# A two-layer decoder trunk in split float32: the first block by all eight products, 384-column blocks first, squares on VectorE, low parts between a norm's steps, buffers that wait for their own bytes

## The chip, the cores and the metric

The kernel runs on one core of a Trainium2 chip. The metric is the device time of one execution in microseconds (us); less is better. A core has five engines that run side by side, each through its own instructions in order: TensorE (PE in the profile; PEld is its loading of the stationary operand), VectorE (DVE), ScalarE (ACT), GpSimd (POOL) and SyncE (SP, which here only issues DMAs). Matmuls accumulate into PSUM, which has eight banks of 128 x 512 float32.

## The reference

x has 512 tokens and 1024 channels, float32. Two layers, each:

```python
x = x + 0.5 * swiglu(rmsnorm(x, ln_ffn1[l]), w_ffn1_gu[l], w_ffn1_down[l])
h = rmsnorm(x, ln_mix[l]);  z = h @ w_in[l]
u_pool, q, k, v, gate_logits = split(z)
a = pool_mixer(u_pool, ...) @ w_pool_branch[l]
b = swa_sink_attention(q, k, v, sinks[l]) @ w_attn_branch[l]
g_pool, g_attn = split(sigmoid(gate_logits))
x = x + (g_pool * a + g_attn * b) @ w_out[l]
x = x + 0.5 * swiglu(rmsnorm(x, ln_ffn2[l]), w_ffn2_gu[l], w_ffn2_down[l])
# swiglu(h): g, u = split(h @ w_gu);  (silu(g) * u) @ w_down
# rmsnorm(x, g): x * rsqrt(mean(x*x) + 1e-6) * g
```

The inner width of a SwiGLU is 2816, so that w_gu has 5632 columns: 2816 for the gate, 2816 for the up part.

## The kernel before

**Split float32.** Every matrix operand is written as a high part (a copy rounded to the fast float32 format, made by ScalarE) and a low part (the difference, made by VectorE). One product of 128 x 128 by 128 x n is three matmuls: high by high, high by low, low by high. `term` (line 272) writes them for most stages; `split` (line 134) makes the parts of an activation: a copy on ScalarE, then a subtraction on VectorE that waits for it.

**Layout.** x lies transposed in SBUF as eight tiles of 128 channels by 512 tokens (k = 0 to 7, "k-tiles").

**SwiGLU** (`ffn`, line 396). The 2816 columns go in six blocks, two to a group, `GROUPS = ((512, 512), (512, 512), (384, 384))` (line 26). A block computes gate and up of its n columns. It takes channels in halves (k-tiles 0 to 3 and 4 to 7), tokens in halves of 256, and gate and up as halves of columns, and uses a Strassen form: seven products instead of eight, named a11, s2, s1, s3, a12, s4, a22 (line 27, `ORDER`; the first block of a SwiGLU goes by `FIRST`, with a12 second). A product is 24 matmuls of n columns: 2 weight chunks (c) x 2 token tiles (q) x 2 k-tiles x 3. They accumulate in three pairs of banks (pt[1], pt[2], pt[3]). Their activation operands, B11, T1, T2, T3, T4, B21 and B22, are halves of the scaled x and differences of them; `Norm.split(k)` (line 315) makes them: for k < 4 B11 and T1, for k >= 4 B21 with B22, T2 with T3, and T4. Behind the products stand small steps on VectorE and ScalarE (p1, p2, q6, q7, p3, a22, lines 443 to 477). p1, behind a11, copies pt[1] to r, and in the first block calls the norm's sums; a12 accumulates on pt[1], so it waits for these copies. q7, behind s3, computes v = P2 - r and then v = v - P3; s4 accumulates on P3, so it waits for that. `turned` (line 490) transposes a finished 128 x n product through the banks pt_tp and pt_pv into hh and hl (high and low part), which the down projection reads; half of the products wait in the list `turns` until `turn()`, behind the next block's a11 or early in `down`.

**down** (line 505): after each group, eight output tiles m, each over the group's 8 (or 6) k-tiles: 24 (or 18) matmuls; then `done` adds half of it to x. In the last group of a SwiGLU `done` also calls `nxt.split(m)` and `nxt.square(m)` for the next norm and then `W.prep()`. Before a norm of a SwiGLU the order of m is `HALVES` = 0, 4, 1, 5, 2, 6, 3, 7.

**The norm's scale.** `square` (line 353): ScalarE squares x, and the squares are added up into ssq, on GpSimd for the norms before a SwiGLU (`halves`), on VectorE for those before the mixer. `sums` (line 363): PE adds ssq over the partitions with eight small matmuls into pt_tp, VectorE makes rstd of it.

**Weights** (class `Weights`, line 146). A plan lists the chunks of 128 x 1024 (or 768) in the order of use. `prep` (line 253), after each used chunk, prepares on: low parts up to 3 chunks ahead (`LO`, three buffers wl), sums of chunks for s2 and s4 on VectorE (`add_up`, buffers sums), high parts up to 4 ahead on ScalarE (`HI`, buffers wh), then loads (six buffers raw). Plain loads go through SP's queue; for s1 and s3 a second load adds up in DMA through GpSimd's queue.

**The mixer** (`mix`, line 552) ends with eight tiles m in the order HALVES of x += y @ w_out, 24 matmuls each, with `nxt.split`, `nxt.square` and `prep` behind each.

**Order.** The class `InOrder` (line 82) keeps each engine's instructions in the order in which the program writes them; no scheduler moves them. All instructions carry line 90, its call, in the profile, so groups are told by their tiles. Pools of buffers (hp, ep, er, sums, the banks pf in `ffn`; mp, rp, ps, psc in `mix`) are opened and closed by each stage.

**The start** (from line 826 on): the loads of x and of the first chunks are written out by hand, then all eight `split` with the first chunks' high and low parts between, then eight `square`; then the first `ffn`.

Of the kernel before, what the change touches and what calls it, by code (L numbers as in the profile page):

```python
# [18 lines left out]
P = 128  # L19
# [6 lines left out]
GROUPS = ((512, 512), (512, 512), (384, 384))  # L26
# [75 lines left out]
def trunk(ctx, tc, xT, consts, vecs, rows, w_g4, w_g3, w_d8, w_d6, w_qkv, w_u, w_pool, w_gate, w_br, w_out, out):  # L102
# [43 lines left out]
    class Weights:  # L146
# [3 lines left out]
        def __init__(self):  # L150
# [3 lines left out]
            for l in range(L):  # L154
                for f in range(2):
# [8 lines left out]
                    for gi, group in enumerate(GROUPS):  # L164
                        for i, n in enumerate(group):
                            w = w_g4[l, f, b] if n == 512 else w_g3[l, f, b - 4]
                            self.block(w, 2 * n, FIRST if b == 0 else ORDER)
                            b += 1
                        last = gi + 1 == len(GROUPS)
                        for m in (HALVES if f == 1 and last else range(KT)):  # L170
                            w = w_d6[l, f, m] if last else w_d8[l, f, gi, m]
                            self.add("dn", 2 * sum(group) // 2, w)
# [136 lines left out]
    class Norm:  # L309
# [5 lines left out]
        def split(self, k):  # L315
# [9 lines left out]
            if not self.halves:  # L325
                split(self.h[:, k, :], self.l[:, k, :], x[:, k, :], scale=g)
                return
            j = k % 4
            of = lambda i, n=1: (t[:, i:i + n, j, :] for t in (self.h, self.l))
            two = lambda t: t.rearrange("p (i t) -> p i t", t=HT)  # L330
            if k < 4:
                split(*of(B11), two(x[:, k, :])[:, 0:1, :], scale=g)
                d = temp("d")[:, :HT]
                nc.vector.tensor_tensor(out=d, in0=x[:, k, :HT], in1=x[:, k, HT:], op=ALU.subtract)
                split(*of(T1), two(d), scale=g)
                return
            xg, t, u = temp("xg"), temp("t23"), temp("t4")[:, :HT]
            gj = self.gain[:, j:j + 1]
            nc.scalar.activation(out=xg, in_=x[:, k, :], func=AF.Copy, scale=g)
            bh, bl = of(B21, 2)  # L340
            nc.scalar.copy(out=bh, in_=two(xg))
# [7 lines left out]
            nc.vector.tensor_tensor(out=bl, in0=two(xg), in1=bh.bitcast(F32), op=ALU.subtract)  # L349
            split(*of(T2, 2), two(t))  # L350
            split(*of(T4), two(u))

        def square(self, k):
# [42 lines left out]
    def ffn(ctx, nm, nxt, last):  # L396
        hp = ctx.enter_context(tc.tile_pool(name="hp", bufs=1))
        ep = ctx.enter_context(tc.tile_pool(name="ep", bufs=1))
        er = ctx.enter_context(tc.tile_pool(name="er", bufs=2))
        W.sums = ctx.enter_context(tc.tile_pool(name="sums", bufs=2))  # L400
        bank["mm"] = ctx.enter_context(tc.tile_pool(name="pf", bufs=6, space=PSUM))
        W.low(W.used + LO)
        W.add_up(W.used + HI + 1)
        W.high(W.used + HI)
        W.low(W.used + LO)
        W.load()
        turns = []

        def block(n, base, hid, order):
# [39 lines left out]
            def p2():  # L449
                sa.update(enumerate(new("sa")))  # L450
                each(lambda q: nc.scalar.activation(out=sa[q], in_=pt[1][q], func=AF.Silu, scale=rs(q)))

            def q6():
                u2.update(enumerate(new("u")))
                each(lambda q: nc.vector.tensor_tensor(out=u2[q], in0=r1[q], in1=pt[2][q], op=ALU.subtract))

            def q7():
# [21 lines left out]
            steps = {"a11": (B11, 1, p1), "s2": (T2, 2, q6), "s1": (T1, 3, None), "s3": (T3, 2, q7),  # L479
                     "a12": (B21, 1, p2), "s4": (B22, 3, p3), "a22": (T4, 2, a22)}  # L480
# [19 lines left out]
        def turn():  # L500
            for t in turns:
                turned(*t)
            turns.clear()

        def down(hid, kts, final, ms):
# [7 lines left out]
            def done(m, pd):  # L513
# [3 lines left out]
                if final:  # L517
                    if nxt is not None:
                        nxt.split(m)
                        nxt.square(m)  # L520
                    if last:
                        nc.sync.dma_start(out=out[m * P:(m + 1) * P, :], in_=x[:, m, :])
# [16 lines left out]
        for gi, group in enumerate(GROUPS):  # L539
            hid = [hp.tile([P, 8, S], F32R, name=n) for n in ("hh", "hl")]  # L540
            base = 0
            for i, n in enumerate(group):
                block(n, base, hid, FIRST if gi == i == 0 else ORDER)
# [8 lines left out]
    def mix(ctx, l, nm, nxt):  # L552
        mp = ctx.enter_context(tc.tile_pool(name="mp", bufs=1))
        rp = ctx.enter_context(tc.tile_pool(name="rp", bufs=RING))
        bank["mm"] = ctx.enter_context(tc.tile_pool(name="ps", bufs=4, space=PSUM))
        psc = ctx.enter_context(tc.tile_pool(name="psc", bufs=1, space=PSUM))
# [261 lines left out]
        for m in HALVES:  # L818
# [3 lines left out]
            nxt.split(m)  # L822
            nxt.square(m)
            W.prep()

    gain = lambda l, i: vec[:, l, i * KT:(i + 1) * KT]
    nm = Norm(gain(0, 0), True)
# [108 lines left out]
```

## Time and profile before

| | |
|---|---|
| time, median of 3 runs | 1981.16 us (1981.11 to 1984.77) |
| profiled execution | 1982.2 us, of it span 1980.2 us |
| mean granted TensorE clock | 0.988 |
| ScalarE busy | 852.2 us (43%) |
| GpSimd busy | 132.9 us (7%) |
| read from HBM | 254.81 MB |

The span runs from the first to the last instruction. The profile lists busy time of each engine, groups of instructions (operation, output<-inputs by the program's names, shapes, count, busy time, mean duration), and for each instruction the idle time of its engine in front of it with the engine and tile that ended it (`[24.09 <-POOL ssq L90]`). "x24" in a line of the timeline or of the chain of waits is a number of instructions merged into it. A matmul's own duration is longer than the distance to the next one, since matmuls are pipelined; its price is the distance.

### The profile page before, as it was taken

How to read it: one execution, taken by the hardware profiler on the slowest of the kernel's cores; microseconds unless marked ns; L12 is line 12 of the kernel's file. 1: busy time of each engine (PE TensorE's matmuls, PEld its weight loads, DVE VectorE, ACT ScalarE, POOL GpSimd, SP SyncE). 2: the span in 40 equal slices, each digit the busy share in tenths (PEclk: the TensorE clock that was granted, in tenths of full speed). 3: DMA queues.
4: the chain of work that ended last, by engine and by line, in shares of the span. 5: the costliest groups of instructions: out<-in, count | busy, mean ns of one | idle time of the engine just before them, and what ended most of it. 6: DMA issues, size and time to landing. Idle time of an engine off the chain costs nothing.

```text
span 1980.2 us, 24215 instructions
## 1 busy us (share of the span) xinstructions
PE 1920.4 (97%) x9240; PEld 1611.0 (81%) x9240; DVE 1304.4 (66%) x1884; ACT 852.2 (43%) x1286; POOL 132.9 (7%) x134
## 2 busy tenths in 40 slices
PE   3999999999999999999989999999999999999999
PEld 2788889897778788889868888898977877888897
DVE  5765747667756774756787476576765677657474
ACT  5433525445534542433454244244454454335242
POOL 3000000000001100000020000000000021000000
PEclk6999999999999999999999999999999999999999
DMA  5655546422224554646546564553222237455452
GB/s 173 178 148 150 160 107 160 128 92 75 75 86 117 149 160 128 181 120 148 134 119 179 140 172 124 127 154 119 90 64 86 85 87 204 139 151 165 117 157 78
DMA packets 77348, 258.48 MB, mean 131 GB/s; under 512 B 8720, under 2 KB 8720, under 8 KB 77232
## 3 DMA queue, kind: packets, MB, share of 16 engines
q1 hardware_dynamic: 63072, 210.27, 32.6%
q0 software_dynamic: 13872, 46.28, 13.9%
q8 instruction: 72, 1.18, 0.3%
q14 instruction: 44, 0.36, 0.1%
q10 hardware_dynamic: 288, 0.39, 0.1%
HBM read 254.81 MB, written 2.10 MB: 130 GB/s over the span
## 4 chain that ended last, share of the span: by engine, by line
PE 92%; DVE 5%; ACT 2%; issue 0%; DMA 0%; POOL 0%; SPq 0%; ACTq 0%; POOLq 0%
PE mm L90 86%; PE sc L90 3%; PE pt_pv L90 2%; PE pt_tp L90 2%; DVE wl L90 2%; DVE xgl L90 1%; ACT xgh L90 1%; DVE x L90 1%; DVE t L90 1%; DMA raw<-in_w_g 0%; DVE ssq L90 0%; ACT wh L90 0%; POOL ssq L90 0%; DVE v L90 0%; ACT xg L90 0%
## 5 line engine op out<-in xcount | busy, mean ns | idle before, releaser
L90 ACT CAST wh<-raw 128x1024 fp32r<-128x1024 f32 (+1 forms) x420 | 417.9, 995 | 567.6 <-PE mm L90 536.3
L90 DVE TENSOR_TENSOR wl<-raw,wh 128x1024 fp32r<-128x1024 f32 (+1 forms) x420 | 495.2, 1179 | 158.7 <-PE mm L90 83.3
L90 PE MATMUL mm<-wh,xgh 128*128 128x512 f32 (+2 forms) x1440 | 532.4, 370 | 25.4 <-DVE x L90 9.0
L90 PE MATMUL mm<-wl,xgh 128*128 128x512 f32 (+2 forms) x1440 | 529.1, 367 | 1.2 <-DVE wl L90 1.2
L90 PE MATMUL mm<-wh,xgl 128*128 128x512 f32 (+2 forms) x1440 | 528.7, 367 | 0.0
L90 PEld LDWEIGHTS mm<-wh,xgh 128*128 128x128 f32 x1440 | 272.7, 189 | 64.4 <-ACT wh L90 21.7
L90 PEld LDWEIGHTS mm<-wl,xgh 128*128 128x128 f32 x1440 | 272.8, 189 | 37.3 <-DVE wl L90 2.0
L90 PEld LDWEIGHTS mm<-wh,xgl 128*128 128x128 f32 x1440 | 272.6, 189 | 35.8
L90 PE MATMUL mm<-hh,wl 128*128 128x512 f32 x704 | 279.9, 398 | 2.6 <-DVE wl L90 2.6
L90 PE MATMUL mm<-hh,wh 128*128 128x512 f32 x704 | 281.6, 400 | 0.0
L90 PE MATMUL mm<-hl,wh 128*128 128x512 f32 x704 | 279.5, 397 | 0.0
L90 DVE SCALAR_TENSOR_TENSOR x<-mm,x 128x512 f32<-128x512 f32 x96 | 66.3, 690 | 215.3 <-PE mm L90 215.3
L90 POOL DMA_DIRECT2D raw<-in_w_g x96 | 82.1, 858 | 1700.9 <-DMA raw<-in_w_g 757.2
L90 ACT CAST wh<-sums 128x1024 fp32r<-128x1024 f32 (+1 forms) x96 | 94.1, 980 | 197.6 <-PE mm L90 140.7
L90 PEld LDWEIGHTS mm<-hh,wl 128*128 128x128 f32 x704 | 133.0, 189 | 35.8 <-DVE wl L90 3.5
L90 PEld LDWEIGHTS mm<-hh,wh 128*128 128x128 f32 x704 | 133.0, 189 | 31.2
L90 PEld LDWEIGHTS mm<-hl,wh 128*128 128x128 f32 x704 | 132.9, 189 | 31.3
L90 PE MATMUL mm<-xgh,wh 128*128 128x512 f32 x384 | 154.8, 403 | 1.8 <-DVE x L90 1.8
L90 PE MATMUL mm<-xgh,wl 128*128 128x512 f32 x384 | 150.1, 391 | 0.0
L90 PE MATMUL mm<-xgl,wh 128*128 128x512 f32 x384 | 149.9, 390 | 0.0
L90 DVE TENSOR_TENSOR wl<-sums,wh 128x1024 fp32r<-128x1024 f32 (+1 forms) x96 | 106.7, 1131 | 12.8 <-PE mm L90 12.6
L90 PEld LDWEIGHTS mm<-xgh,wh 128*128 128x128 f32 x384 | 72.1, 188 | 22.5 <-issue 8.2
(174 smaller groups left out, 1979.6 us busy)
## 6 DMA issues: line engine op xcount, KB each, us to landing
raw<-in_w_g SPq DMA_DIRECT2D x160, 512.0 KB, 3.9
raw<-in_w_g POOLq DMA_DIRECT2D x64, 512.0 KB, 6.2
raw<-in_w_d SPq DMA_DIRECT2D x64, 512.0 KB, 3.4
raw<-in_w_g SPq DMA_DIRECT2D x80, 384.0 KB, 3.2
raw<-in_w_gate SPq DMA_DIRECT2D x32, 512.0 KB, 3.5
raw<-in_w_g POOLq DMA_DIRECT2D x32, 384.0 KB, 5.1
raw<-in_w_d SPq DMA_DIRECT2D x32, 384.0 KB, 3.1
raw<-in_w_br SPq DMA_DIRECT2D x16, 512.0 KB, 3.5
```

The source lines that it names most:

```text
L90: return lambda *args, **kw: self.tc.keep_in_program_order(call(*args, **kw))
```

## The change

- **First block plain.** In the first SwiGLU of layer 0 the first block is made by all eight products (`plain`), straight from the halves of x (`split_plain`), first all gate columns, then all up columns, with accumulators for four token tiles at once; pt_tp and pt_pv are two of them in the second half. The differences T1 to T4, which the later blocks need, are made behind the four chunks of the second half (`first`, `others`). The first chunk comes in two loads.
- **384-column blocks first.** `GROUPS` starts with (384, 384); the last group, behind which the next norm's operands are made, is (512, 512).
- **Squares on VectorE** before every norm.
- **Low parts between a norm's steps.** `split` gets a function `between`, called between the high part on ScalarE and the low part on VectorE; in `done` and at the end of the mixer it is `W.prep`.
- **v** takes P3 in a step p5 behind s1 (v = r + P3), and q7 becomes v = P2 - v. The norm's sums move from behind a11 to behind the first block's second kind with a step q6 (s2); two of `turns` are transposed behind each of the first two products.
- **Buffers that wait for their own bytes.** The pools of `ffn` and `mix` get `reuse_waits="tile"`; without it a pool that is opened on another's memory waits for the whole earlier pool.

```diff
-GROUPS = ((512, 512), (512, 512), (384, 384))
+GROUPS = ((384, 384), (512, 512), (512, 512))
...
-    def split(hi, lo, src, scale=None):
+    def split(hi, lo, src, scale=None, between=lambda: None):
         if scale is None:
             nc.scalar.copy(out=hi, in_=src)
+            between()
             nc.vector.tensor_tensor(out=lo, in0=src, in1=hi.bitcast(F32), op=ALU.subtract)
...
+                            plain = l == f == 0
+                            if plain and b == 0:
+                                for j in range(2):
+                                    for c in range(4):
+                                        self.add("plain", 2 * n, w[j, c])
+                            else:
+                                self.block(w, 2 * n, FIRST if b == int(plain) else ORDER)
...
+            else:
+                xg = self.scaled(k)
+                bh, bl = self.of(B21, k - 4, 2)
+                nc.scalar.copy(out=bh, in_=halves(xg))
+                between()
+                self.others(k - 4, xg, lambda: nc.vector.tensor_tensor(
+                    out=bl, in0=halves(xg), in1=bh.bitcast(F32), op=ALU.subtract
+                ))
...
+        def split_plain(self, k, b12):
...
+            if k < 4:
+                split(*self.of(B11, k), halves(x[:, k, :])[:, 0:1, :], scale=g)
+                split(*(t[:, k:k + 1, :] for t in b12), halves(x[:, k, :])[:, 1:2, :], scale=g)
+            else:
+                split(*self.of(B21, k - 4, 2), halves(x[:, k, :]), scale=g)
...
-                e = nc.gpsimd if self.halves else nc.vector
-                e.tensor_tensor(out=self.acc, in0=self.acc, in1=sq, op=ALU.add)
+                nc.vector.tensor_tensor(out=self.acc, in0=self.acc, in1=sq, op=ALU.add)
...
-        hp = ctx.enter_context(tc.tile_pool(name="hp", bufs=1))
+        hp = ctx.enter_context(tc.tile_pool(name="hp", bufs=1, reuse_waits="tile"))
...
             def p1():
                 r1.update(enumerate(new("r", er)))
                 each(lambda q: nc.scalar.copy(out=r1[q], in_=pt[1][q]))
-                if nm.rstd is None:
-                    nm.sums()
...
             def q6():
                 u2.update(enumerate(new("u")))
                 each(lambda q: nc.vector.tensor_tensor(out=u2[q], in0=r1[q], in1=pt[2][q], op=ALU.subtract))
+                if nm.rstd is None:
+                    nm.sums()
+                    gate()
+
+            def p5():
+                v.update(enumerate(new("v")))
+                each(lambda q: nc.vector.tensor_tensor(out=v[q], in0=r1[q], in1=pt[3][q], op=ALU.add))

             def q7():
-                v.update(enumerate(new("v")))
-                each(lambda q: nc.vector.tensor_tensor(out=v[q], in0=pt[2][q], in1=r1[q], op=ALU.subtract))
-                each(lambda q: nc.vector.tensor_tensor(out=v[q], in0=v[q], in1=pt[3][q], op=ALU.subtract))
+                each(lambda q: nc.vector.tensor_tensor(out=v[q], in0=pt[2][q], in1=v[q], op=ALU.subtract))
...
-                if kind == "a11":
+                if kind in order[:2]:
                     turn()
...
+        def plain(n, base, hid):
+            b12 = [sums.tile([P, 4 * HT], F32R, name="sums").rearrange("p (k t) -> p k t", k=4) for _ in range(2)]
+            pts = [mm()[:, :n] for _ in range(6)]
+            for k in range(KT):
+                nm.split_plain(k, b12)
+                if k % 2 == 0:
+                    W.high(k // 2 + 1)
+                    W.low(k // 2 + 1)
+            for k in range(KT):
+                nm.square(k)
+            act = []
+            for j in range(2):
+                if j:
+                    pts = pts[4:] + [pa.tile([P, S], F32, name=name)[:, :n] for name in ("pt_tp", "pt_pv")]
+                for c in range(4):
+                    wh, wl = (t[:, :2 * n].rearrange("p (k f) -> p k f", k=2) for t in W.take("plain"))
...
+                            term(pts[b], kt, KT, ah, al, wh[:, k, :], wl[:, k, :])
+                    if j == 0 and c == 3:
+                        nm.sums()
...
+                    W.prep()
+                    if j:
+                        nm.first(c)
+                        nm.others(c, nm.scaled(c + 4))
+            for b in range(NB):
+                u = (er if b < 2 else ep).tile([P, 512], F32, name=("r0", "r1", "v0", "v1")[b])[:, :n]
+                nc.vector.scalar_tensor_tensor(
+                    out=u, in0=pts[b], scalar=nm.rstd[:, b:b + 1], in1=act[b], op0=ALU.mult, op1=ALU.mult
+                )
+                turns.append((u, b, base, n, hid, b % 2))
...
-                if final:
-                    if nxt is not None:
-                        nxt.split(m)
-                        nxt.square(m)
+                if final and nxt is not None:
+                    nxt.split(m, W.prep)
+                    nxt.square(m)
+                    return
...
-    loads = iter(W.loads[2:RAW])
+    loads = iter(W.loads[1:RAW])
     for k in range(KT):
         nc.sync.dma_start(out=x[:, k, :], in_=xT[k * P:(k + 1) * P, :])
-        if k in (1, 3, 5):
+        if k < 2:
+            c = W.loads[0]
+            cols = slice(k * c["n"] // 2, (k + 1) * c["n"] // 2)
+            nc.sync.dma_start(out=c["raw"][:, cols], in_=c["src"][:, cols])
+        elif k % 2 == 0:
             W.issue(next(loads))
...
```

More of the change, by code (lines that the diff above doesn't have):

```diff
@@ L313, in __init__, with split @@
             self.h = self.rstd = None
-        def split(self, k):
+        def split(self, k, between=lambda: None):
             g = self.gain[:, k:k + 1]
@@ L325, in split, with of, scaled, first @@
             if not self.halves:
[L326 to L337, printed above, removed]
+                split(self.h[:, k, :], self.l[:, k, :], x[:, k, :], scale=g, between=between)
+            elif k < 4:
+                split(*self.of(B11, k), halves(x[:, k, :])[:, 0:1, :], scale=g, between=between)
+                self.first(k)
+            else:
+                xg = self.scaled(k)
+                bh, bl = self.of(B21, k - 4, 2)
+                nc.scalar.copy(out=bh, in_=halves(xg))
+                between()
+                self.others(k - 4, xg, lambda: nc.vector.tensor_tensor(
+                    out=bl, in0=halves(xg), in1=bh.bitcast(F32), op=ALU.subtract
+                ))
+        def of(self, i, j, n=1):
+            return [t[:, i:i + n, j, :] for t in (self.h, self.l)]
+        def scaled(self, k):
+            xg = temp("xg")
+            nc.scalar.activation(out=xg, in_=x[:, k, :], func=AF.Copy, scale=self.gain[:, k:k + 1])
+            return xg
+        def first(self, j):
+            d = temp("d")[:, :HT]
+            nc.vector.tensor_tensor(out=d, in0=x[:, j, :HT], in1=x[:, j, HT:], op=ALU.subtract)
+            split(*self.of(T1, j), halves(d), scale=self.gain[:, j:j + 1])
+        def others(self, j, xg, between=lambda: None):
+            t, u = temp("t23"), temp("t4")[:, :HT]
             gj = self.gain[:, j:j + 1]
-            nc.scalar.activation(out=xg, in_=x[:, k, :], func=AF.Copy, scale=g)
-            bh, bl = of(B21, 2)
-            nc.scalar.copy(out=bh, in_=two(xg))
             nc.vector.scalar_tensor_tensor(
@@ L348, in split @@
             nc.vector.tensor_tensor(out=u, in0=xg[:, :HT], in1=t[:, :HT], op=ALU.subtract)
-            nc.vector.tensor_tensor(out=bl, in0=two(xg), in1=bh.bitcast(F32), op=ALU.subtract)
-            split(*of(T2, 2), two(t))
-            split(*of(T4), two(u))
+            between()
+            split(*self.of(T2, j, 2), halves(t))
+            split(*self.of(T4, j), halves(u))
+        def split_plain(self, k, b12):
+            g = self.gain[:, k:k + 1]
+            if self.h is None:
+                self.h, self.l = (
+                    xp.tile([P, 7 * 4 * HT], F32R, name=n).rearrange("p (i k t) -> p i k t", i=7, k=4)
+                    for n in ("xgh", "xgl")
+                )
[4 more added lines that the diff above has]
+                split(*self.of(B21, k - 4, 2), halves(x[:, k, :]), scale=g)
         def square(self, k):
@@ L445, in p1, with gate @@
                 each(lambda q: nc.scalar.copy(out=r1[q], in_=pt[1][q]))
-                if nm.rstd is None:
-                    nm.sums()
             def p2():
+                if nm.rstd is not None:
+                    gate()
+            def gate():
                 sa.update(enumerate(new("sa")))
@@ L477, in a22 @@
                 ))
-            steps = {"a11": (B11, 1, p1), "s2": (T2, 2, q6), "s1": (T1, 3, None), "s3": (T3, 2, q7),
+            steps = {"a11": (B11, 1, p1), "s2": (T2, 2, q6), "s1": (T1, 3, p5), "s3": (T3, 2, q7),
                      "a12": (B21, 1, p2), "s4": (B22, 3, p3), "a22": (T4, 2, a22)}
@@ L542, in ffn @@
             for i, n in enumerate(group):
-                block(n, base, hid, FIRST if gi == i == 0 else ORDER)
+                if nm is first and gi == i == 0:
+                    plain(n, base, hid)
+                else:
+                    fresh = W.sums is None
+                    if fresh:
+                        open_sums()
+                    block(n, base, hid, FIRST if fresh else ORDER)
                 base += n // P
```

88 lines of the change are left out of this document (45 added, 43 removed).

## The prediction

> **What bounds the kernel now.** I read the page first, then what TensorE (PE) waits for, then the chain of work that ended last, then the timeline where the chain leaves PE.
>
> ```profile
> span 1980.2 us, 24215 instructions
> ...
> PE 1920.4 (97%) x9240; PEld 1611.0 (81%) x9240; DVE 1304.4 (66%) x1884; ACT 852.2 (43%) x1286; POOL 132.9 (7%) x134
> ```
>
> PE is busy for 97% of the span: a gain can only come from stretches in which PE stands still or runs at a low clock, and every product that is added costs its full time. The waits of PE show where it stands:
>
> ```profile
> PE pt_tp L90 <- POOL ssq L90: 24.1, 1, 24.1
> PE mm L90 <- DVE x L90: 10.8, 5, 7.3
> PE mm L90 <- DVE v L90: 5.9, 4, 1.5
> ...
> PE mm L90 <- DVE wl L90: 3.8, 4, 2.3
> ```
>
> One wait of 24.1 us stands at the start; the others sit beside the norms. The chain gives PE's paces, and one of the waits for v:
>
> ```profile
> 70.77 1.30 DVE v L90 x2
> ...
> 90.55 32.67 PE mm L90 x144
> ...
> 329.30 24.99 PE mm L90 x144
> ...
> 967.07 4.21 PE mm L90 x18
> ```
>
> A matmul of 512 columns takes 32.67/144 = 0.227 us, one of 384 columns 24.99/144 = 0.174, one of the down projection 4.21/18 = 0.234. So a product (24 matmuls) takes 5.45 us at 512 columns and 4.16 at 384; one down step of six k-tiles takes 4.2 us, one of eight (24 matmuls) 5.6.
>
> The timeline of the start:
>
> ```profile
> 9.59 1.05 ACT L90 CAST wh<-raw 128x1024 fp32r<-128x1024 f32 x1 [3.81 <-DMA raw<-in_w_g]
> ...
> 10.68 0.80 PE L90 MATMUL mm<-wh,xgh 128*128 128x512 f32 x1 [5.80 <-ACT wh L90]
> ...
> 12.20 0.42 DVE L90 TENSOR_TENSOR d<-x 128x256 f32<-128x256 f32 x1
> ...
> 13.20 0.48 DVE L90 SCALAR_TENSOR_TENSOR xgl<-d,vec,xgh 128x256 fp32r<-128x256 f32 x1 [0.58 <-ACT xgh L90]
> ...
> 19.10 0.48 DVE L90 SCALAR_TENSOR_TENSOR t<-x,vec,xg 128x256 f32<-128x256 f32 x1
> ...
> 20.48 0.68 DVE L90 TENSOR_TENSOR xgl<-xg,xgh 128x512 fp32r<-128x512 f32 x1
> ...
> 21.08 1.02 DVE L90 TENSOR_TENSOR xgl<-t,xgh 128x512 fp32r<-128x512 f32 x2
> ...
> 32.12 11.96 POOL L90 TENSOR_TENSOR ssq<-ssq,sq 128x512 f32<-128x512 f32 x7 [10.90 <-ACT sq L90]
> ...
> 44.13 1.87 PE L90 MATMUL pt_tp<-ones,ssq 128*128 128x1 f32 x8 [24.09 <-POOL ssq L90]
> ...
> 45.86 0.77 PE L90 MATMUL mm<-wh,xgh 128*128 128x512 f32 x1
> ```
>
> PE does one product from 10.68 to 20, then stands before the norm's sums: ScalarE and VectorE are making all seven operands of the Strassen form for eight k-tiles until 32, and GpSimd adds seven squares in 11.96 us behind that. The second product starts at 45.86.
>
> Then VectorE's own work: low parts of 768 and 1024 columns (one of them under an addition on GpSimd), the addition of a square on GpSimd and on VectorE, and the product with the gate at 384 columns.
>
> ```profile
> 979.26 0.95 DVE L90 TENSOR_TENSOR wl<-raw,wh 128x768 fp32r<-128x768 f32 x1
> ...
> 984.53 2.80 DVE L90 TENSOR_TENSOR wl<-raw,wh 128x768 fp32r<-128x768 f32 x1
> ...
> 1011.27 1.22 DVE L90 TENSOR_TENSOR wl<-raw,wh 128x1024 fp32r<-128x1024 f32 x1
> ```
>
> ```profile
> L90 POOL TENSOR_TENSOR ssq<-ssq,sq 128x512 f32<-128x512 f32 x28 | 48.6, 1735 | 75.2 <-ACT sq L90 74.8
> ```
>
> ```profile
> L90 DVE TENSOR_TENSOR ssq<-ssq,sq x14: 684/685/689, 369.2 to 1364.8; 128x512 f32<-128x512 f32 x14
> ```
>
> ```profile
> L90 DVE SCALAR_TENSOR_TENSOR r<-r,rstd,sa 128x384 f32<-128x384 f32 x2 | 1.1, 612 | 0.0
> ```
>
> Then PE behind a wait, at the boundary of the layers, and VectorE's and ScalarE's steps between PE's last matmul of the mixer and a12 of the next block:
>
> ```profile
> 987.39 0.80 PE L90 MATMUL mm<-hh,wl 128*128 128x512 f32 x1 [2.33 <-DVE wl L90]
> 987.98 0.63 PE L90 MATMUL mm<-hh,wh 128*128 128x512 f32 x1
> 988.41 0.63 PE L90 MATMUL mm<-hl,wh 128*128 128x512 f32 x1
> ```
>
> ```profile
> 1013.24 0.77 PE L90 MATMUL mm<-wh,xgh 128*128 128x512 f32 x1 [7.26 <-DVE x L90]
> ```
>
> ```profile
> 651.19 0.70 DVE x L90
> ...
> 657.98 1.15 DVE sums L90
> ...
> 659.20 1.05 ACT wh L90
> 660.25 0.49 ACT r L90
> ...
> 660.78 22.07 PE mm L90 x96
> ```
>
> Behind a wait of only 2.33 us the matmuls start 0.43 us apart instead of 0.23: PE's clock has dropped.
>
> **The change, part by part.** *Start.* Of the first product of the plain block PE needs one chunk and two tiles of x. The chunk comes in two pieces between x's first tiles; in the trace the first chunk is there at 9.59 with both tiles long there. I let PE start at 10.7 as before (8.5 to 13). The eight products of a block are 8 x 24 x 0.174 = 33.3 us, one product (4.2) more than seven. The first half takes 16.7, and about 2 more at the low clock (ten matmuls by 0.2): to 29.4. Splits and squares are done by then: VectorE has about 7 us of splits (by 0.48 for 256 columns at 13.20), 3.8 of low parts of chunks (0.95 each) and 7 additions of 0.69, and even stretched by the arrival of x to 25 us they end ahead of PE; the wait of 24.1 goes. The sums cost PE 1 us, the second half goes from 30.4 to 47.
>
> Late next is VectorE in that second half. Behind each of its four chunks stand a low part (0.95) and one k-pair of differences. From the rows: the pair's first part takes 12.20 to 13.68 = 1.5; the second 19.10 to 22.10 = 3.0, less 0.6 for the low part of B21 and B22 that split_plain has made; the copy before it 0.3 more. That is 4.2, with the low part 5.15 a chunk against PE's 4.16. And it begins only when PE has done the first chunk of this half (34.6), because the low part in front of it needs that chunk's buffer (three of them). So VectorE ends at 34.6 + 4 x 5.15 = 55.2, and the four products with the gate, 0.57 each, at 57.5. PE does a11 of the next block until 51.2 and then comes to the transposes of these products, in pt_tp and pt_pv, which the plain block's third and fourth accumulator still hold: it waits until about 57. Then a12 waits for the copies of P1 on ScalarE, which stand behind the cast of the first s2 sum, which waits for VectorE's addition: 57.5 + 0.95 + 0.8 + 0.5 = 59.7, and some 2 us of low clock. Balance: at 61.7 PE has done 216 matmuls of 384 columns, 37.5 us, of which 33.3 are useful; before, it had by 45.86 done one product of 5.45, and 2 of low clock and 1.5 of waiting for v were still to come, so by 49.4. 27.9 us more work in 12.3 us more time: **-15.6**. Bounds: no stall at the transposes, -26; x or VectorE 8 us later than worked out, -8.
>
> *Norm steps.* The boundary of the layers is the place where VectorE sets the pace:
>
> ```profile
> 976.18:987.26 11.08, 8.87 (x38) 6.78 (x36) 9.05 (x14) 5.81 (x10) 2.14 (x2) 0.99 0.43 91
> ```
>
> A pair of steps takes VectorE 11.08 us, 9.05 of it busy and 2.0 waiting for ScalarE's high parts; PE needs 8.4 for the pair. One low part took 2.80 where the same shape takes 0.95: it lies under a GpSimd addition. With the change VectorE's pair is 9.05 - 1.85 + 2 x 0.27 (wider low parts) + 2 x 0.69 (squares) = 9.1 plus about 0.7 of gaps, since the low parts fill most of them; PE's pair is 11.2 with eight k-tiles. VectorE is hidden, and at the last step it starts when PE ends.
>
> Before, PE loses there 2.3 + 7.3 in waits, and after each starts at 0.43 us a matmul instead of 0.23: six and ten such matmuls, 1.3 and 2.2 us. In all 13.1. What stays is the way to a12, shown above from 651.19 on. From PE's last matmul to a12 are 9.8 us, of which PE fills 5.45 with a11 and 0.9 with the sums (1.87 at the low clock): 3.4 lost. With the change VectorE needs for the last step x 0.7, low part 0.95, differences and low parts 3.0 (19.10 to 22.10), square 0.69, with gaps 5.5; then sum 0.95, cast 0.8, copy 0.5: a12 starts after 7.8. But a11 is now 4.2 long and the sums come later: 3.6 lost, and 1.3 of low clock, 4.9. Boundary of the layers: 4.9 - 13.1 = **-8.2** (-4 if VectorE stays behind by one step, -11 if a12 comes straight after a11). Mixer to SwiGLU, twice: 4.9 against 3.4 and at most 2 of low clock, taken as **+1** together (-4 to +8).
>
> The page "TensorE: Matmul & The Clock Gate", section "What's actually happening", of the Trainium skill says that the clock halves only after an idle window of about 3.4 us. By it the wait of 2.33 us would have left the clock whole; the rows at 987.98 and 988.41 stand 0.43 apart, so here it did not, and the measurement decides. By the page alone my waits of 3.6 us lie at the edge, and without low clock behind three of them the time would be some 4 us lower.
>
> *v.* s4 no longer waits, since v takes P3 up right after s1, with a product between: three waits of 1.5 besides the one counted above: **-4.4** (0 if VectorE is late there).
>
> *Buffers that wait for their own bytes.* The four waits for x of (10.8 - 7.3)/4 = 0.9: the first accumulators of the new pool were last read some steps earlier, so two of them at the mixer go, **-1.8**; the two at the SwiGLU are in its 3.4 already. Bounds 0 and -3.5.
>
> *Order of the groups and fewer loads* leave the same columns and bytes; steps of eight k-tiles where six stood cover VectorE, and the six go where no norm is made. At nothing: a down step of six k-tiles gives VectorE 4.2 us for x and one low part, 1.6. SP's queue gets x and the chunks in another order, which the start holds; GpSimd's queue loses the additions that its weight loads stood behind.
>
> Sum: -15.6 - 8.2 + 1 - 4.4 - 1.8 = -29. The profiled execution took 1982.2 (span 1980.2, 2.0 around it), 1.0 above the median of 1981.2. So 1982.2 - 29 - 1.0 = **1952**.
>
> **Rivals.** *The differences hide* (no stall at the transposes): start -26, 1942. For it: VectorE idles in the first half; against: the order of its queue is written out. Chance 0.15. *VectorE stays the bound in the norm steps*: gaps stay (2.0 a pair) and the additions come on top, 11.1 against 11.2, so the last step ends later; three boundaries lose 3 more each and the start 3: 1964. Chance 0.2. *The pool edges stay*, so that the reuse does not do what it says: +3.5, 1955; chance 0.05. *Slower*: the squares and the low parts make VectorE the bound in all 24 steps before the three Strassen norms. To undo 29 us a step must exceed 5.6 by 1.2, from 6.8 us on it decides; at 7.1 the time is 1952 + 24 x 1.5 = 1988. The pair of 11.08, 5.5 a step with the GpSimd stretch in it, speaks against it. Chance 0.04.
>
> **The numbers.** Forecast 0.56, the rest as above. The range 1938 to 1968 holds the forecast with its bounds, the hidden differences and the bound VectorE; outside lie the slower case and the corners of the others. 0.2% (4 us) is about what a measurement can tell from no change; all cases but one lie further below: faster 0.95, same 0.01, slower 0.04.
>
> **What would show it.** The wait for ssq gone, PE starting near 10.7 and broken by one wait of 5 to 9 us near 50, for transposes and then the copies of P1; the layers' boundary with one wait of some 3.6 us before a12, none for x or wl in the down steps; no PE wait for v. Wrong would be a wait for ssq or for the first chunks of more than 3 us, VectorE without gaps in the norm steps, or new waits in blocks far from a norm.

## The result and the profile after

The changed kernel takes 1951.21 us (median of 4 runs, 1948.64 to 1952.40) where the kernel before takes 1981.13 (4 runs, 1980.42 to 1984.77): a ratio of 0.9844, 95% interval 0.9827 to 0.9861. The forecast was 1952. The profiled execution took 1951.35 us, its span 1949.6, its mean granted TensorE clock 0.995 (before: 1982.2, 1980.2 and 0.988).

The page's head and busy times (busy us, share of the span, instructions):

```profile
span 1949.6 us, 24211 instructions
...
PE 1921.7 (99%) x9264; PEld 1617.6 (83%) x9264; DVE 1297.0 (67%) x1896; ACT 844.3 (43%) x1282; POOL 82.5 (4%) x102
```

The 24 matmuls more are the eighth product; the span is 30.6 us shorter all the same, so PE's empty time has fallen by more than that. What PE waits for (us in total, times, longest):

```profile
PE mm L90 <- ACT r L90: 10.8, 4, 3.2
PE pt_tp L90 <- DVE v L90: 6.4, 1, 6.4
PE mm L90 <- ACT wh L90: 5.2, 1, 5.2
PE pt_pv L90 <- DVE warm_in L90: 1.1, 1, 1.1
PE mm L90 <- DVE wl L90: 0.3, 1, 0.3
```

The 24.1 us for ssq are gone, so are all waits for x and for v in a product, and the 3.8 for wl are 0.3. What is left of any size is PE's first wait for data (wh, 5.2), one new wait of 6.4 for v at the transposes, and four waits for r, the copies of P1: 1.14 at the start and 3.2 at each of the three boundaries before a later Strassen norm.

To see what low clock adds to the waits, I added up for both traces, over all matmuls, how much longer the distance to the next one is than the median distance for its shape (0.227, 0.173 or 0.234 us for the three large shapes). Called lost time here, in us:

| stretch | before | after | difference |
|---|---|---|---|
| start, 0 to 80 us | 38.8 | 19.0 | -19.8 |
| boundary of the layers (60 us) | 14.5 | 5.2 | -9.3 |
| two boundaries mixer to SwiGLU (40 us each) | 9.5 | 10.6 | +1.1 |
| three later waits for v | 4.9 | 0 | -4.9 |
| two waits for x at the mixers' starts | 2.1 | 0 | -2.1 |
| all of the span | 87.0 | 52.2 | -34.8 |

The eighth product costs 24 x 0.173 = 4.15; -34.8 + 4.15 = -30.6, the difference of the spans. The rows above the last leave 0.2 for the rest of the span.

The timeline of VectorE in the second half of the plain block and behind it:

```profile
31.70 0.16 DVE L90 TENSOR_SCALAR rs_v<-pt_tp 128x4 f32<-128x4 f32 x1 [4.11 <-PE pt_tp L90]
...
37.76 0.42 DVE L90 TENSOR_TENSOR d<-x 128x256 f32<-128x256 f32 x1
...
42.88 0.42 DVE L90 TENSOR_TENSOR d<-x 128x256 f32<-128x256 f32 x1
...
53.13 0.41 DVE L90 TENSOR_TENSOR d<-x 128x256 f32<-128x256 f32 x1
...
57.37 1.14 DVE L90 SCALAR_TENSOR_TENSOR r<-mm,rstd,sa 128x384 f32<-128x384 f32 x2
...
58.95 0.60 DVE L90 SCALAR_TENSOR_TENSOR v<-pt_pv,rstd,u 128x384 f32<-128x384 f32 x1
```

A chunk takes VectorE 42.88 - 37.76 = 5.12 us, and three of them lie between 37.76 and 53.13. The first half ends with rstd at 31.7, the products with the gate stand from 57.4 to 59.5. PE behind that:

```profile
59.09 0.90 PE L90 MATMUL pt_tp<-cst,r 128*128 128x128 f32 x3 [6.40 <-DVE v L90]
...
61.77 0.69 PE L90 MATMUL mm<-wh,xgh 128*128 128x384 f32 x1 [1.14 <-ACT r L90]
```

PE waits 6.40 us for the last of these products and then 1.14 for the copies: a12 starts at 61.77.

The boundary of the layers, as the timeline of PE shows it:

```profile
988.73 0.34 PE L90 MATMUL mm<-wh,xgl 128*128 128x384 f32 x1
992.32 0.45 PE L90 MATMUL mm<-wh,xgh 128*128 128x384 f32 x1 [3.25 <-ACT r L90]
992.60 0.34 PE L90 MATMUL mm<-wl,xgh 128*128 128x384 f32 x1
...
993.16 0.52 PE L90 MATMUL mm<-wl,xgh 128*128 128x384 f32 x1
993.48 0.52 PE L90 MATMUL mm<-wh,xgl 128*128 128x384 f32 x1
993.80 0.52 PE L90 MATMUL mm<-wh,xgh 128*128 128x384 f32 x1
```

Where before two waits stood in and behind the down steps, a single wait of 3.25 us stands before a12; from 0.84 us behind it the matmuls are 0.32 us apart instead of 0.174, which costs about another 1.75.

### The profile page after: what moved, and what is told of

It is laid out like the page before. It is cut to its first block, busy times and chain, and to the rows that moved or that the text cites. A ratio compares the mean times of both kernels' runs of the same rounds, so it can differ in the third digit from the quotient of the medians.

```text
span 1949.6 us, 24211 instructions
## 1 busy us (share of the span) xinstructions
PE 1921.7 (99%) x9264; PEld 1617.6 (83%) x9264; DVE 1297.0 (67%) x1896; ACT 844.3 (43%) x1282; POOL 82.5 (4%) x102
## 4 chain that ended last, share of the span: by engine, by line
PE 96%; DVE 2%; DMA 1%; ACT 1%; issue 0%; SPq 0%; ACTq 0%; DVEq 0%; POOLq 0%
PE mm L90 89%; PE sc L90 3%; PE pt_pv L90 2%; PE pt_tp L90 2%; DMA raw<-in_w_g 1%; DVE wl L90 0%; DVE t L90 0%; DVE xgl L90 0%; ACT wh L90 0%; ACT xgh L90 0%; DVE sums L90 0%; DVE r L90 0%; DVE x L90 0%; ACT xg L90 0%; DVE ssq L90 0%
## 5 line engine op out<-in xcount | busy, mean ns | idle before, releaser
L90 DVE TENSOR_TENSOR wl<-raw,wh 128x1024 fp32r<-128x1024 f32 (+1 forms) x418 | 479.8, 1148 | 130.7 <-PE mm L90 87.6
L90 PE MATMUL mm<-wh,xgh 128*128 128x512 f32 (+2 forms) x1424 | 526.5, 370 | 16.1 <-ACT r L90 10.8
L90 PE MATMUL mm<-wl,xgh 128*128 128x512 f32 (+2 forms) x1424 | 523.7, 368 | 0.3 <-DVE wl L90 0.3
(203 smaller groups left out, 1981.3 us busy)
```

Source lines behind the costliest of these rows:

```text
L90: return lambda *args, **kw: self.tc.keep_in_program_order(call(*args, **kw))
```

## The experiments

Each differs from the changed kernel by the edit shown. All times are medians of 4 runs; in the same sessions the kernel before took 1981.1 (e1 to e4), 1981.3 (e5 to e8) and 1982.1 (e9 to e11). The theory: the gain is PE's empty time, most of it at the start and at the boundary of the layers, where making the low parts early keeps VectorE hidden; what is left is the two stalls that the forecast named. A note for reading the traces: in the profiled runs with the same loads at the start (all but e1, e5 and e11) PE's first product begins anywhere from 9.38 (e7) to 10.89 us (e2), so two spans can differ by 1.5 us for that alone. Rivals: the gain comes from squares off GpSimd or from the pools rather than from the plain block and the order of the steps.

### e1: the first block by seven products again

```diff
-                            plain = l == f == 0
+                            plain = False
...
+    for k in range(4):
+        nm.split(k)
...
+    for k in range(4, KT):
+        nm.split(k)
```

(with the loads and the order of splits of the start before)

> The change without the plain block: the first block by the seven products, all operands made at the start as before; groups, squares on VectorE, low parts, v and pools as changed. My theory: ScalarE has the copies of P1 queued behind all splits and squares, so a12 starts near 37 us, PE stands some 18 us from about 18.5 on, and the kernel takes about 1958 us, 7 above the changed kernel: half of the 13 to 15 us at the start come from moving the sums behind s2 and the squares to VectorE. Rival (the plain block carries the whole gain of the start): 1965 or more. Rival (the squares carry it): within 2 us of the changed kernel.

1958.68 us (1956.98 to 1959.02), ratio 0.9883 [0.9868, 0.9898]. In the waits of PE:

```profile
PE mm L90 <- ACT r L90: 28.0, 4, 18.3
```

a11 is issued by 19.57 and a12 starts at 38.43: the wait of 24.1 comes back as one of 18.3, now for the copies. The plain block alone is worth 1958.68 - 1951.21 = 7.5 us by the medians, about half of the start's gain of 15.6. In the traces the first mixer starts 9.3 us later than in the changed kernel (382.67 against 373.33), and the rest of the run is 2.1 shorter, 1.5 of it because no slow matmuls follow the wait at the boundary of the layers. The other half came to this kernel too: its wait is 5.8 shorter than before's 24.1, though its first block is made by seven products as well. What this kernel has there beside the old start are squares on VectorE, sums two products later (behind s2, the third product) and a block of 384 columns; which of them does it was not separated. The traces speak for the later sums: PE asks for them only at 49.41 here, and in the kernel before GpSimd's squares were ready at 44.13. That is an argument, and no run has the later sums alone.

### e2: the SwiGLU norms' squares on GpSimd again

```diff
-                nc.vector.tensor_tensor(out=self.acc, in0=self.acc, in1=sq, op=ALU.add)
+                e = nc.gpsimd if self.halves else nc.vector
+                e.tensor_tensor(out=self.acc, in0=self.acc, in1=sq, op=ALU.add)
```

> The changed kernel with the squares added up on GpSimd before the SwiGLU norms, as before. My theory: hidden now, since VectorE has about 1.4 us of slack a pair of steps; stretched low parts of 2 to 2.8 us come back (three or four a norm) but PE does not wait for them in the down steps; at the start the seven additions take 12 us and end near 31, about when PE asks for the sums: 1951, within 3 us. Rival (the additions on GpSimd are a main cost): 1956 or more, with PE waits for x or wl in the down steps or for ssq.

1953.09 us (1952.58 to 1955.06), 0.9859 [0.9844, 0.9873]. The waits of PE:

```profile
PE mm L90 <- ACT r L90: 12.2, 4, 3.7
```

No wait for ssq, x or wl comes back; the copies are waited for up to 0.5 longer at each boundary. 1.9 us are too little to be told from none. But the run does not bring the old clash back. VectorE's low parts stand at another place of a step now, and of those before the three later norms only three, all at the boundary of the layers, are stretched under a GpSimd addition, the longest to 2.00 us where its shape takes 1.22 elsewhere:

```profile
964.40 2.00 DVE L90 TENSOR_TENSOR wl<-raw,wh 128x1024 fp32r<-128x1024 f32 x1
```

In the kernel before ten were stretched at these three places, to between 2.05 and 2.80. So e2 shows that the additions may stay on GpSimd once the low parts have moved. What they cost in the old order of a step was not run.

### e3: the low parts behind a norm's step, not between

```diff
-                    nxt.split(m, W.prep)
+                    nxt.split(m)
                     nxt.square(m)
+                    W.prep()
```

(and so at the end of the mixer)

> The changed kernel with the preparation of weights behind a norm's step again, not between its high and low parts. My theory: VectorE's pair of steps goes from 9.5 to about 11.2 us, level with PE's 11.2, and the last step before a12 gets 1 to 1.5 us longer at three places: 1955, 3 to 5 above the changed kernel, the waits of PE for the copies r at 4.5 instead of 3.2. Rival (eight k-tiles alone hide it, the order inside a step is worth nothing): within 1 us. Rival (VectorE falls behind over the eight steps): 1960 or more, with PE waits for x or wl.

1958.65 us (1957.77 to 1959.51), 0.9885 [0.9870, 0.9899]: 7.4 above the changed kernel, more than the 3 to 5 expected. The waits of PE, and VectorE's steps in the timeline:

```profile
PE mm L90 <- ACT r L90: 15.2, 4, 5.9
...
PE mm L90 <- DVE wl L90: 1.8, 2, 1.5
```

```profile
956.30 0.69 DVE L90 SCALAR_TENSOR_TENSOR x<-mm,x 128x512 f32<-128x512 f32 x1
...
957.78 0.48 DVE L90 SCALAR_TENSOR_TENSOR t<-x,vec,xg 128x256 f32<-128x256 f32 x1 [0.80 <-ACT xg L90]
...
967.38 0.68 DVE L90 SCALAR_TENSOR_TENSOR x<-mm,x 128x512 f32<-128x512 f32 x1
```

VectorE waits 0.80 for ScalarE again within the step, and a pair of steps takes it 967.38 - 956.30 = 11.08 us, against PE's 11.2. The table of stretches (window, us, then busy us of PE, PEld, VectorE, ScalarE and GpSimd, each with its instructions) has such a pair of e3 first and of the changed kernel below:

```profile
956.30:967.38 11.08, 11.08 (x49) 8.88 (x49) 9.02 (x17) 6.25 (x10) 0.86 (x1) 1.00 0.44 108
...
954.74:964.25 9.51, 9.51 (x42) 7.66 (x41) 8.82 (x17) 6.23 (x11) 0.86 (x1) 1.00 0.59 153
```

VectorE is busy 9.02 us of its pair in e3 and 8.82 in the changed kernel: the work is nearly the same, and the gaps are 2.06 against 0.69. That is what the low parts between the steps do.

Level with PE is not hidden. In the changed kernel seven steps lie between VectorE's first addition to x at 951.20 and its last, for which it waits for PE, at 984.94: 33.7 us, which is five steps of 5.6 and two of 2.8, so PE ends the first ones faster than it goes on (`down` begins three tiles with their first halves). A VectorE that is no faster than PE carries the lag that it gets there to the end: in e3 its last addition comes at 989.38, 37.3 us behind its first. The wait before a12 at the boundary of the layers grows from 3.25 to 5.9, and 1.5 for a low part comes in. At the two mixers' ends the wait grows from 3.2 to 4.1. My estimate had counted the gaps and not this lag, which was the last rival's. With 7.4 us this part is worth as much as the plain block by the medians.

### e4: without reuse_waits

```diff
-        hp = ctx.enter_context(tc.tile_pool(name="hp", bufs=1, reuse_waits="tile"))
+        hp = ctx.enter_context(tc.tile_pool(name="hp", bufs=1))
```

(and so for the other eight pools)

> The changed kernel with pools that wait for the whole earlier pool. My theory: a wait for x of 0.9 us comes back at each of five stage borders; at the two mixer starts it costs 0.9 each, before the three SwiGLU norms it lies under the wait for a12: 1953, 1 to 3 above the changed kernel. Rival (the borders cost nothing now): same and no wait for x. Rival (other buffers of the new pools wait as well): 1956 or more.

1951.89 us (1948.62 to 1953.19), 0.9853 [0.9836, 0.9869]: no difference to be told. The waits of PE, and PE's timeline at the first mixer's end:

```profile
PE mm L90 <- ACT r L90: 7.5, 4, 2.1
PE mm L90 <- DVE x L90: 4.4, 5, 0.9
```

```profile
640.40 0.34 PE L90 MATMUL mm<-wh,xgl 128*128 128x384 f32 x1
642.87 0.45 PE L90 MATMUL mm<-wh,xgh 128*128 128x384 f32 x1 [2.13 <-ACT r L90]
...
643.50 0.34 PE L90 MATMUL mm<-wh,xgh 128*128 128x384 f32 x1
643.67 0.34 PE L90 MATMUL mm<-wl,xgh 128*128 128x384 f32 x1
```

The five waits for x are back, as expected, two at mixer starts and three at SwiGLU starts. At the latter the time was due anyway: the wait for x takes 0.9 from the wait for r that follows, 3.2 becoming 2.13. And behind the shorter wait the matmuls go on at 0.174: the slow matmuls, which follow all three single waits of the changed kernel and cost 1.6 to 1.8 us each time, followed none of the three split ones. So in these two profiled runs the 2 us gained at the mixers' starts were given back through the clock. It is no fixed rule: in the kernel before, one of two waits split in the same way was followed by nine slow matmuls (at 1634.12), and of the twelve single waits of 3.2 us in the traces of four kernels (the changed one, e1, e6 and e9) three were followed by none.

### e5: the 384-column group last

```diff
-GROUPS = ((384, 384), (512, 512), (512, 512))
+GROUPS = ((512, 512), (512, 512), (384, 384))
```

(and the weights laid out to match)

> The changed kernel with the groups in the old order (512, 512, 384 columns last), the plain block with 512 columns. My theory: before the norm at the border of the layers VectorE's pair of steps (about 9.3 us) is above PE's 8.4, which brings back 3 to 6 us there; the wait at the first transposes shrinks from 6.4 to about 3, the three waits before a12 by 0.5 each, the eighth product costs 1.3 more: 1952, 1949 to 1956. Rival (the order of the groups is a main part of the gain): 1959 or more.

1953.91 us (1950.98 to 1954.49), 0.9856 [0.9841, 0.9871]. The waits of PE:

```profile
PE mm L90 <- ACT r L90: 15.3, 4, 7.7
...
PE pt_tp L90 <- DVE v L90: 1.9, 1, 1.9
```

The longest wait, at the boundary of the layers, grows from 3.25 to 7.7 us, where steps of six k-tiles give VectorE 4.2 us and not 5.6; the one at the transposes falls from 6.4 to 1.9, where a product of 512 columns gives it 5.45 and not 4.16. The two nearly cancel, as expected: by the medians the order is worth 2.7 us, of which the eighth product at 512 columns is 1.3 by its pace, and the runs of the two kernels overlap. It trades one stall for the other.

### e6 and e7: the two stalls that stayed

The wait of 6.4 us has a cause in the order of VectorE's queue (all differences behind the second half's chunks). e6 puts two of the four pairs into the first half:

```diff
-                    if j:
-                        nm.first(c)
-                        nm.others(c, nm.scaled(c + 4))
+                    d = {(0, 1): 0, (0, 2): 1, (1, 0): 2, (1, 1): 3}.get((j, c))
+                    if d is not None:
+                        nm.first(d)
+                        nm.others(d, nm.scaled(d + 4))
```

> The changed kernel with the four k-pairs of differences made behind chunks 2 and 3 of the plain block's first half and chunks 1 and 2 of its second, instead of behind the four of the second half. My theory (VectorE's 5.1 us a chunk make PE wait at the transposes): VectorE is done ahead of PE, the wait of 6.4 us goes, a wait for the copies r of about 1.5 stays, and some low clock goes: 1943, 6 to 9 below the changed kernel. Rival (something else holds the transposes): wait of 4 us or more stays, 1949 or more.

1944.13 us (1942.98 to 1947.05), 0.9812 [0.9797, 0.9827]: 7.1 less, and the wait for v is gone from PE's waits. A wait of 2.8 for the norm's rstd has come, since VectorE has more to do ahead of the sums:

```profile
PE mm L90 <- ACT r L90: 10.1, 4, 3.2
PE pt_tp L90 <- DVE rs_v L90: 2.8, 1, 2.8
```

The waits of 3.2 for r name ScalarE's copies, but the copies themselves are short. The timeline of ScalarE in the changed kernel at the boundary of the layers shows why they come late:

```profile
988.58 0.63 ACT L90 ACTIVATE sq<-x 128x512 f32<-128x512 f32 x1
991.05 0.83 ACT L90 CAST wh<-sums 128x768 fp32r<-128x768 f32 x1 [1.84 <-DVE sums L90]
991.79 0.85 ACT L90 COPY r<-mm 128x384 f32<-128x384 f32 x2
```

ScalarE stands idle for 1.84 us in front of the high part of the first s2 sum, which VectorE makes behind all its norm work, and the copies are queued behind it though they need only PE's result. e7 lets `prep` leave high parts out between a11's chunks and makes them behind the copies:

```diff
-        def prep(self):
+        def prep(self, hold=False):
...
-            self.high(self.used + HI)
+            if not hold:
+                self.high(self.used + HI)
...
                     if c == 0:
-                        W.prep()
+                        W.prep(kind == "a11" and order[1] == "a12")
```

> The changed kernel with the high parts of s2 made only behind the copies of P1 in a SwiGLU's first seven-product block. My theory (the copies stand on ScalarE behind a cast that waits for VectorE): the three waits of 3.2 us before a12 and the low clock behind them go, a wait of up to 1 us for s2's parts comes: 1941, 7 to 12 below the changed kernel. Rival (a12 waits for something else that ends then, such as its own low parts): 2 to 3 us of wait stay at each place, 1948 or more.

1942.48 us (1941.11 to 1942.52), 0.9799 [0.9783, 0.9815]: 8.7 less. ScalarE at the same place, and the waits of PE:

```profile
984.78 0.63 ACT L90 ACTIVATE sq<-x 128x512 f32<-128x512 f32 x1
985.32 0.84 ACT L90 COPY r<-mm 128x384 f32<-128x384 f32 x2
987.20 0.84 ACT L90 CAST wh<-sums 128x768 fp32r<-128x768 f32 x1 [1.04 <-DVE sums L90]
```

```profile
PE pt_tp L90 <- DVE v L90: 7.0, 2, 6.4
PE mm L90 <- ACT r L90: 1.6, 3, 0.6
```

The copies follow straight on the square, the three waits of 3.2 fall to 1.6 in all, and the start's wait of 6.4 stays, as it should. Six waits for low parts, 2.3 in all, have come. That the queue in front of the copies held PE is thereby shown; the prediction had named this queue ("stand behind the cast of the first s2 sum") but taken it as given.

### e8: both

> Both edits together. My theory: they add up, 1932, 15 to 21 below the changed kernel, PE waits below 12 us in all, most of it for the first chunk. Rival (they share a wait): no more than 12 below.

1937.16 us (1935.60 to 1940.55), 0.9777 [0.9761, 0.9793]: 14.0 less by the medians, where 15 to 21 were expected, and 15.8 by the spans (1949.6 to 1933.8). The two gains add up (7.1 + 8.7 = 15.8) but for the measurement's spread; what stays is the wait for rstd:

```profile
PE pt_tp L90 <- DVE rs_v L90: 3.3, 1, 3.3
```

### e9: v as before, behind s3 alone

```diff
-            def p5():
...
             def q7():
-                each(lambda q: nc.vector.tensor_tensor(out=v[q], in0=pt[2][q], in1=v[q], op=ALU.subtract))
+                v.update(enumerate(new("v")))
+                each(lambda q: nc.vector.tensor_tensor(out=v[q], in0=pt[2][q], in1=r1[q], op=ALU.subtract))
+                each(lambda q: nc.vector.tensor_tensor(out=v[q], in0=v[q], in1=pt[3][q], op=ALU.subtract))
...
```

> The changed kernel with v in its old form: both subtractions behind s3, none behind s1. My theory: s4 waits again for v in each SwiGLU's first seven-product block, four waits of 1.0 to 1.5 us at 384 columns: 1956, 4 to 6 above the changed kernel. Rival (another place takes the wait up, so that v is worth nothing): within 1 us of it.

1954.32 us (1953.38 to 1956.40), 0.9859 [0.9844, 0.9874]: 3.1 above, with the four waits of 1.2 that were expected:

```profile
PE mm L90 <- DVE v L90: 4.8, 4, 1.2
```

The waits are there in full; the time rose by less than the 4 to 6 expected. The profiled run, 2.0 longer than the changed kernel's, shows where some of it went: PE began 1.24 us earlier (9.50 against 10.74), and one of the three boundaries had no slow matmuls, which makes up for some 1.5. Without these two the four waits would cost about 4.7, an estimate from the two traces.

### e10 and e11: what is next at the start

e10 is e8 with the second pair of differences behind the first half's last chunk, so that fewer of them stand ahead of the sums:

```diff
-                    d = {(0, 1): 0, (0, 2): 1, (1, 0): 2, (1, 1): 3}.get((j, c))
+                    d = {(0, 1): 0, (0, 3): 1, (1, 0): 2, (1, 1): 3}.get((j, c))
```

> Copies of P1 first and differences early, with the differences of the second k-pair behind the sums' scale (chunk 4 of the first half) and the last two behind chunks 1 and 2 of the second half. My theory: PE's wait of 3.3 us for the scale's read of pt_tp and the low clock behind it go, up to 1 us stays at the first transposes: 1933, 3 to 5 below the kernel with both edits. Rival (the wait only moves to the transposes): within 1 us of it.

1935.47 us (1935.04 to 1936.56), 0.9764 [0.9748, 0.9781]: 1.7 below e8, less than the 3 to 5 expected and too little to be told from none. The wait for rstd went, and waits for low parts, which grew from 2.0 to 3.6 in all, took part of its place:

```profile
PE mm L90 <- ACT wh L90: 5.8, 3, 5.4
PE mm L90 <- DVE wl L90: 3.6, 8, 1.0
```

The first line is PE's start. e11 is e10 with the load of `row` (136 KB, one copy to each partition, used first by the mixer) issued on SP's queue behind the first chunks, no more at the very start on GpSimd's:

```diff
-    nc.gpsimd.dma_start(out=row, in_=rows.rearrange("l n -> (l n)").partition_broadcast(P))
...
+    nc.sync.dma_start(out=row, in_=rows.rearrange("l n -> (l n)").partition_broadcast(P))
```

> The same with the broadcast load of the row constants moved from GpSimd's queue at the very start to SP's queue behind the first chunks and x. My theory: between 4.3 and 6.5 us the DMA engines are busy with that broadcast, so the first chunk lands some 2 us earlier and PE starts near 8.5 instead of 10.7: 1931, 2 us lower. Rival (the first chunk waits for something else): no earlier start, 1933.

1930.48 us (1929.97 to 1934.47), 0.9742 [0.9727, 0.9756]: the best version, 50.7 below the kernel before's 1981.13 and 5.0 below e10, where 2 were expected. Its start in the timeline, and the same two lines of the changed kernel:

```profile
6.51 0.83 ACT L90 CAST wh<-raw 128x768 fp32r<-128x768 f32 x1 [1.81 <-DMA raw<-in_w_g]
7.39 0.69 PE L90 MATMUL mm<-wh,xgh 128*128 128x384 f32 x1 [1.89 <-ACT wh L90]
```

```profile
9.86 0.83 ACT L90 CAST wh<-raw 128x768 fp32r<-128x768 f32 x1 [5.18 <-DMA raw<-in_w_g]
10.74 0.69 PE L90 MATMUL mm<-wh,xgh 128*128 128x384 f32 x1 [5.24 <-ACT wh L90]
```

PE starts 3.35 us earlier, outside the 9.38 to 10.89 of the other runs. The profiled run is the longest of its four (1934.47), and its span of 1932.6 is only 0.6 below e10's 1933.2: slow matmuls take 0.7 of the earlier start at once, and the first blocks of two later SwiGLUs take another 2, with waits of 0.2 to 0.3 and slower matmuls at the transposes. So the earlier start is shown, and that it lasts to the end is shown by the other three runs' times alone.

## Why the prediction was right, point by point

- **Start: -15.6 forecast, about -15.6 measured** (-19.8 of lost time, +4.15 for the eighth product). The steps hold one by one: PE starts at 10.74 (10.7), a chunk's worth of differences takes VectorE 5.12 (5.15), the products with the gate begin at 57.37 (end of the four at 57.5 forecast, 59.5 measured), the wait lies at the transposes, then at the copies, a12 at 61.77 (59.7). The two later moments and the later end of the first half, rstd at 31.70 (30.4), are errors of 1 to 2 us. PE loses 3.3 us in the first half to slow matmuls and a short wait for a low part, where 2 stood in the sum; behind a12 the low clock costs 1.3 and not 2. That the start comes out to 0.1 us is luck, since PE's first product alone comes up to 1.4 us earlier in other runs. e6 shows that the stall at the transposes was VectorE's order and not its load, which is the first rival's mechanism: the differences would hide, had they been written earlier.
- **What part of the start's gain is whose** was not in the prediction. e1 shows 7.5 us for the plain block by the medians and 9.3 in the traces; the rest of it comes also with the seven products.
- **Boundary of the layers: -8.2 forecast, -9.3 measured** (lost time 14.5 and 5.2 against the working's 13.1 and 4.9). VectorE's pair of steps takes 9.51, 8.82 busy and 0.69 of gaps (9.1 and 0.7 forecast), and is hidden under PE's 11.2. The bound-VectorE rival falls with that, and e3, which makes its condition, shows its price: 7.4. e3 also shows that the low parts between are what fills the gaps. The 1.85 that the working took from the GpSimd additions' stretching stands as a reading of the trace before; e2 does not test it, since the low parts have moved away from most additions.
- **Mixer to SwiGLU: +1 forecast, +1.1 measured.** Waits of 3.2 us each (3.6 forecast), and 1.6 to 1.8 of low clock behind each (1.3). e7 shows that the wait was the order of ScalarE's queue.
- **v: -4.4 forecast;** PE's waits for v in a product went from 5.9 to 0, the three beside the start's are 4.9 of lost time, and e9 puts the price of all four at 3.1 by the medians, about 4.7 by its trace.
- **Buffers: -1.8 forecast, no gain shown.** This step failed: the waits for x went from 10.8 to 0, of which the two at the mixers' starts are 2.1 as worked out, but e4 without the edit is no slower that can be told (1951.89 to 1951.21). The step counted waits and left out that at the three SwiGLU starts the small wait split the one before a12, behind which the clock then stayed whole in e4's trace. A smaller version of the pool rival (+3.5) also falls: +0.7.
- **The slower case** needed VectorE to bind in 24 steps at 6.8 us or more each; a step takes it 9.51/2 = 4.8.

The five rows of the table differ from their terms by about 0, -1.1, +0.1, -0.5 and -0.3, so the sum is close: 29 forecast, 30.6 by the spans, 29.9 by the medians.

The rule that the prediction weighed, from the Trainium skill's page "TensorE: Matmul & The Clock Gate", section "What's actually happening", sets the clock's drop behind an idle window of about 3.4 us. Here a single wait of 3.2 us was followed by slow matmuls at nine of twelve places (all three of the changed kernel, two of three in each of e1, e6 and e9), and a wait of 0.9 followed some 4 us later by one of 2.1 to 2.3 at one of five (none of three in e4, one of two in the kernel before); the single wait of 2.33 in the kernel before was followed by them. So the length of a wait near the rule's figure does not settle it, and the working's 1.3 us behind each was nearer than the page's zero.

## What to carry to other kernels

When PE is busy for 97% of the span, list its waits one by one and ask of each which queue stands before the named releaser: here a short copy waited behind a cast that itself waited for another engine, and moving it (e7) was worth about as much as the plain block. An engine that shares a steady loop has to be faster than the bound one, not level with it, or a lag from the loop's first steps lasts to its end (e3). A small wait removed in front of a larger one brought nothing here, and in the traces it cost the clock as well (e4).

## What the runs showed of the hardware

- The clock's drop can come after the work has resumed: behind the 3.25 us at the boundary of the layers the first matmuls start 0.28, 0.18, 0.17 and 0.21 apart, and from 993.16 on, 0.84 us after the first, they are 0.32 apart (granted clock 0.95 from 992.30 to 993.16 and 0.53 from there to 996.70). Behind the 3.22 us at 641.62 they are slow from the first on (granted clock 0.50). It lasts for 10 to 11 matmuls in this trace, and for 9 to 12 behind the waits of 3.2 in e1, e6 and e9. Why some waits of this length are followed by it and others not, I have not settled.
- A load that gives every partition a copy of one row (136 KB on the page, used first by the mixer), issued at 1.28 us on GpSimd's queue, went with slow transfers on the other queues: the next x tile, the first chunk's second half and the constants took 7.2 to 7.7 us from issue to landing, and 3.8 to 4.3 when the row was loaded behind them (e11). Between 4.3 and 6.5 us the DMA engines moved 164 GB/s in e10 and 372 in e11. The chunk landed at 9.8 and then at 6.43. In the runs e7 and e9, where the row took 4.8 and 5.2 us to land and not 6.8, the chunk was there by 8.5. Whether it was the queue, the copies or the order in the DMA engines wasn't separated.
- The medians of e10 and e11 differ by 5.0, more than the 3.35 of the earlier start. The profiles do not account for it, since the one of e11 is of its longest run; the runs of e11 lie between 1929.97 and 1934.47, and the 1.7 left over is smaller than that spread.
